# RMSNorm with GELU in float32: the stores of the output moved from ScalarE's hardware queue to GpSimd's software queue

## The chip, the cores and the metric

The kernel runs on one core of a Trainium2 chip. The metric is device time in microseconds (us); each figure is the median of several executions, with lowest and highest behind it where that matters. A single core has no second die to be compared with, so an execution is called fast or slow only by this: slow means more than 1.5% above the fastest execution of the same kernel. "The profile" is one execution recorded by the hardware profiler.

## The reference

```python
def reference(x, gamma, eps):            # x: 8 x 1024 x 2048 float32
    rms = np.sqrt(np.mean(x ** 2, axis=-1, keepdims=True) + eps)
    out = gamma * x / rms
    return 0.5 * out * (1 + np.tanh(np.sqrt(2 / np.pi) * (out + 0.044715 * out ** 3)))
```

The input has 67.11 MB and so has the output. Each row of 2048 numbers needs one sum of squares, a factor and one GELU.

## The kernel before

The 8192 rows are cut into G = 16 tiles of 128 partitions by 4 rows (4 MB each). Six buffers ("slots") hold them, and a tile is computed in place: load, squares on ScalarE, reciprocal root on GpSimd, multiplication by gamma on VectorE, GELU on ScalarE, store. A tile's row of 4 x 2048 numbers is contiguous on both sides, 32 KB.

```python
    slot = [sbuf.tile([P, R, D], FP32, name=f"slot{i}") for i in range(SLOTS)]   # SLOTS = 6
    store_pieces = {G - 1: [(0, 2), (2, 2)]}       # only the last tile is stored in two halves

    def load(g):
        nc.sync.dma_start(out=slot[g % SLOTS], in_=x3[g])                        # line 61

    def gelu_store(g):
        for r, n in store_pieces.get(g, [(0, R)]):
            for q in range(r, r + n):
                nc.scalar.activation(..., func=ACT.Gelu_apprx_tanh,              # line 101
                                     scale=rstd[:, g, q : q + 1])
            nc.scalar.dma_start(                                                 # line 105
                out=o3[g, :, r : r + n, :], in_=slot[g % SLOTS][:, r : r + n, :]
            )
    ...
        for g in range(G + 1):
            if g < G:
                squares(g); inverse_rms(g); scale(g)    # ScalarE line 65; GpSimd; VectorE line 75
            if g:
                gelu_store(g - 1)
                if g - 1 + SLOTS < G:
                    load(g - 1 + SLOTS)                 # waits until the slot has been stored
```

Of the kernel before, what the change touches and what calls it, by code (L numbers as in the profile page):

```python
# [1 line left out]

# [4 lines left out]

FP32 = mybir.dt.float32
ALU = mybir.AluOpType
ACT = mybir.ActivationFunctionType  # L10

P = 128
ROWS = 4
SLOTS = 6

GW = 128


@with_exitstack
def kernel(  # L20
    ctx: ExitStack,
    tc: tile.TileContext,
    x: bass.AP,
    gamma: bass.AP,
    eps: bass.AP,
    out: bass.AP,
):




    nc = tc.nc
    D = x.shape[-1]
    R = ROWS
    eps_f = float(eps)
    x3 = x.rearrange("b s d -> (b s) d").rearrange("(g p r) d -> g p r d", p=P, r=R)
    o3 = out.rearrange("b s d -> (b s) d").rearrange("(g p r) d -> g p r d", p=P, r=R)
    G = x3.shape[0]

    sbuf = ctx.enter_context(tc.tile_pool(name="sbuf", bufs=1))  # L40
    psum = ctx.enter_context(
        tc.tile_pool(name="psum", bufs=1, space=bass.MemoryType.PSUM)
    )
    slot = [sbuf.tile([P, R, D], FP32, name=f"slot{i}") for i in range(SLOTS)]
    gamma_row = sbuf.tile([1, D // GW, GW + 16], FP32, name="gamma_row")
    ones = sbuf.tile([1, P], FP32, name="ones")
    warm = sbuf.tile([1, 1], FP32, name="warm")
    power = sbuf.tile([P, R], FP32, name="power")
    ssq = sbuf.tile([P, G, R], FP32, name="ssq")
    rstd = sbuf.tile([P, G, R], FP32, name="rstd")  # L50
    ms = sbuf.tile([P, R], FP32, name="ms")
    y = sbuf.tile([P, R], FP32, name="y")
    z = sbuf.tile([P, R], FP32, name="z")
    gamma_ps = psum.tile([P, D], FP32, name="gamma_ps")
    junk = psum.tile([P, D], FP32, name="junk")

    store_pieces = {G - 1: [(0, 2), (2, 2)]}
    scale_pieces = {G - 1: [(0, 1), (1, 1), (2, 1), (3, 1)]}

    def load(g):  # L60
        nc.sync.dma_start(out=slot[g % SLOTS], in_=x3[g])  # L61

    def squares(g):
        for r in range(R):
            nc.scalar.activation(  # L65
                out=junk,
                in_=slot[g % SLOTS][:, r, :],
                func=ACT.Square,
                accum_out=ssq[:, g, r : r + 1],
            )  # L70

    def scale(g):
        for r, n in scale_pieces.get(g, [(0, R)]):
            rows = slot[g % SLOTS][:, r : r + n, :]
            nc.vector.tensor_tensor(  # L75
                out=rows,
                in0=rows,
                in1=gamma_ps.unsqueeze(1).to_broadcast([P, n, D]),
                op=ALU.mult,
            )  # L80

    def inverse_rms(g):

        v = nc.gpsimd
        v.tensor_scalar(  # L85
            out=ms, in0=ssq[:, g, :], scalar1=1.0 / D, scalar2=eps_f,
            op0=ALU.mult, op1=ALU.add,
        )
        v.tensor_tensor(out=y, in0=ms, in1=power, op=ALU.pow)  # L89
        v.tensor_tensor(out=z, in0=y, in1=y, op=ALU.mult)  # L90
        v.tensor_tensor(out=z, in0=z, in1=ms, op=ALU.mult)  # L91
        v.tensor_scalar(  # L92
            out=z, in0=z, scalar1=-0.5, scalar2=1.5, op0=ALU.mult, op1=ALU.add
        )
        v.tensor_tensor(out=rstd[:, g, :], in0=z, in1=y, op=ALU.mult)  # L95
# [4 lines that stand above are left out]
                row = slot[g % SLOTS][:, q, :]  # L100
                nc.scalar.activation(  # L101
                    out=row, in_=row, func=ACT.Gelu_apprx_tanh,
                    scale=rstd[:, g, q : q + 1],
                )
            nc.scalar.dma_start(  # L105
                out=o3[g, :, r : r + n, :], in_=slot[g % SLOTS][:, r : r + n, :]
            )

    with tc.manual_schedule():
        for g in range(SLOTS):  # L110
            load(g)
        nc.scalar.dma_start(
            out=gamma_row[:, :, 0:GW],
            in_=gamma.rearrange("(o a b) -> o a b", o=1, b=GW),
        )
        nc.gpsimd.memset(power, -0.5)  # L116
        nc.vector.memset(warm, 0.0)  # L117
        nc.vector.memset(ones, 1.0)  # L118
        nc.scalar.activation(out=warm, in_=warm, func=ACT.Gelu_apprx_tanh)  # L119
        for k in range(0, D, 512):  # L120
            nc.tensor.matmul(  # L121
                out=gamma_ps[:, k : k + 512],
                lhsT=ones,
                rhs=gamma_row[:, k // GW : (k + 512) // GW, 0:GW],
                start=True,
                stop=True,
            )
        for g in range(G + 1):
            if g < G:
                squares(g)  # L130
                inverse_rms(g)
                scale(g)
# [3 lines that stand above are left out]
                    load(g - 1 + SLOTS)  # L136


# [1 line left out]
_INS = ['x', 'gamma', 'eps']  # L140
_OUTS = [((8, 1024, 2048), 'float32')]

_NUMBERS = {'eps': 9.999999747378752e-06}


# [26 lines left out]
```

## Time and profile before

| what | before |
|---|---|
| time | 317.68 us (317.36 to 317.83, 3 runs) |
| span of the profiled execution | 316.9 us |
| rate of the DMA engines, 100 to 260 us | 432 GB/s |
| ScalarE (ACT) busy | 79% |
| GpSimd (POOL) busy | 10% |
| last load landed | 276.2 us |

The table is to be read from the DMA rate: all 16 DMA engines are busy from the first microseconds to 313 us, and the bytes divided by the rate give the time.

### The profile page before, as it was taken

Reading aid. Unit: us, or ns where it says so; the run is one execution under the profiler, and the core shown is the slowest. Engines: PE = TensorE matmul, PEld = TensorE weight load, DVE = VectorE, ACT = ScalarE, POOL = GpSimd, SP = SyncE. Lnnn points to the kernel's source line nnn. Section 1 sums busy time; section 2 is a strip of 40 time slices with the busy share of each in tenths; the row PEclk is TensorE's granted clock in tenths of the full one; section 3 lists DMA queues with packets and bytes.
Section 4 is the critical chain, followed back from the end, with each engine's and each line's share of the span. In section 5 each row is a group of like instructions: output and inputs, shape, how many; then the busy total and the mean of one; then the engine's idle time right before and its main releaser. Section 6 shows DMA issues by size and latency. Waiting matters only on the chain.

```text
span 316.9 us, 473 instructions
## 1 busy us (share of the span) xinstructions
PE 7.2 (2%) x8; PEld 2.5 (1%) x8; DVE 139.4 (44%) x21; ACT 251.1 (79%) x194; POOL 32.3 (10%) x101
## 2 busy tenths in 40 slices
PE   0900000000000000000000000000000000000000
PEld 0300000000000000000000000000000000000000
DVE  0038909090919191732808246091550905582000
ACT  1379999999999997959689595995959859599800
POOL 0020102020202020202002020020200102001000
DMA  8999999999999999999999999999999999999995
GB/s 328 414 451 426 434 393 459 401 459 402 459 405 455 426 434 431 430 434 426 438 426 455 410 455 418 443 426 430 434 430 435 422 459 405 459 414 447 422 420 230
DMA packets 4787, 134.25 MB, mean 424 GB/s; under 512 B 544, under 2 KB 560, under 8 KB 560
## 3 DMA queue, kind: packets, MB, share of 16 engines
q1 hardware_dynamic: 2304, 67.11, 49.5%
q10 hardware_dynamic: 2480, 67.12, 49.1%
q14 instruction: 3, 0.02, 0.0%
HBM read 67.12 MB, written 67.11 MB: 424 GB/s over the span
## 4 chain that ended last, share of the span: by engine, by line
DMA 56%; ACT 33%; issue 5%; ACTq 1%; SPq 0%
DMA slot<-in_x_dram 30%; DMA out_dram<-slot 26%; ACT slot L101 19%; ACT junk L65 14%; ACTq L105 1%; SPq L61 0%; ACTq L101 0%; ACTq L65 0%
## 5 line engine op out<-in xcount | busy, mean ns | idle before, releaser
L75 DVE TENSOR_TENSOR slot<-slot,gamma_ps 128x8192 f32<-128x8192 f32 (+1 forms) x19 | 139.2, 7340 | 147.0 <-ACT junk L65 147.0
L65 ACT ACTIVATE junk<-slot 128x2048 f32<-128x2048 f32 x64 | 120.4, 1881 | 47.3 <-DMA slot<-in_x_dram 43.7
L101 ACT ACTIVATE slot<-slot,rstd 128x2048 f32<-128x2048 f32 x64 | 122.8, 1989 | 0.9 <-ACT slot L101 0.9
L85 POOL TENSOR_SCALAR ms<-ssq 128x4 f32<-128x4 f32 x16 | 3.1, 194 | 247.5 <-ACT junk L65 247.5
L89 POOL TENSOR_TENSOR y<-ms,power 128x4 f32<-128x4 f32 x16 | 16.1, 1009 | 1.3
L65 ACT ACTIVATION_READ_ACCUMULATOR junk<-slot 128x1 f32 x64 | 12.0, 188 | 0.0
L121 PE MATMUL gamma_ps<-gamma_row,ones 1*128 1x512 f32 x8 | 7.2, 1072 | 8.4 <-DMA gamma_row<-in_gamma_dram 8.4
L95 POOL TENSOR_TENSOR rstd<-z,y 128x4 f32<-128x4 f32 x16 | 3.2, 201 | 1.3
L91 POOL TENSOR_TENSOR z<-z,ms 128x4 f32<-128x4 f32 x16 | 3.2, 201 | 1.3
L90 POOL TENSOR_TENSOR z<-y 128x4 f32<-128x4 f32 x16 | 3.2, 199 | 1.3
L92 POOL TENSOR_SCALAR z<-z 128x4 f32<-128x4 f32 x16 | 3.1, 194 | 1.4
L121 PEld LDWEIGHTS gamma_ps<-gamma_row,ones 1*128 1x128 f32 x8 | 2.5, 325 | 11.5 <-issue 11.5
L119 ACT ACT_TABLE_LOAD x1 | 1.3, 1283 | 1.3 <-PEq L153 1.3
L117 DVE MEMSET warm<- 1x1 f32 x1 | 0.1, 59 | 0.8 <-PEq L153 0.8
L119 ACT ACTIVATE warm<-warm 1x1 f32<-1x1 f32 x1 | 0.2, 202 | 0.0
L118 DVE MEMSET ones<- 1x128 f32 x1 | 0.2, 165 | 0.0
L116 POOL MEMSET power<- 128x4 f32 x1 | 0.1, 102 | 0.3 <-POOLq L153 0.3
L153 POOL MEMSET const-float32-0.0<- 128x1 f32 x1 | 0.1, 99 | 0.2 <-issue 0.2
L153 POOL MEMSET const-bfloat16-1.0<- 128x1 bf16 x1 | 0.1, 102 | 0.0
L153 POOL MEMSET const-uint8-127<- 128x1 uint8 x1 | 0.1, 102 | 0.0
L153 POOL MEMSET const-float32-1.0<- 128x1 f32 x1 | 0.1, 99 | 0.0
## 6 DMA issues: line engine op xcount, KB each, us to landing
slot<-in_x_dram SPq DMA_DIRECT2D x16, 4096.0 KB, 37.1
out_dram<-slot ACTq DMA_DIRECT2D x15, 4096.0 KB, 38.6
out_dram<-slot ACTq DMA_DIRECT2D x2, 2048.0 KB, 15.0
gamma_row<-in_gamma_dram ACTq DMA_DIRECT2D x1, 8.0 KB, 7.5
```

Source lines behind the costliest of these rows:

```text
L65: nc.scalar.activation(out=junk, in_=slot[g % SLOTS][:, r, :], func=ACT.Square, accum_out=ssq[:, g, r : r + 1],)
L75: nc.vector.tensor_tensor(out=rows, in0=rows, in1=gamma_ps.unsqueeze(1).to_broadcast([P, n, D]), op=ALU.mult,)
L85: v.tensor_scalar(out=ms, in0=ssq[:, g, :], scalar1=1.0 / D, scalar2=eps_f, op0=ALU.mult, op1=ALU.add,)
L89: v.tensor_tensor(out=y, in0=ms, in1=power, op=ALU.pow)
L90: v.tensor_tensor(out=z, in0=y, in1=y, op=ALU.mult)
L91: v.tensor_tensor(out=z, in0=z, in1=ms, op=ALU.mult)
L92: v.tensor_scalar(out=z, in0=z, scalar1=-0.5, scalar2=1.5, op0=ALU.mult, op1=ALU.add)
L95: v.tensor_tensor(out=rstd[:, g, :], in0=z, in1=y, op=ALU.mult)
L101: nc.scalar.activation(out=row, in_=row, func=ACT.Gelu_apprx_tanh, scale=rstd[:, g, q : q + 1],)
L105: nc.scalar.dma_start(out=o3[g, :, r : r + n, :], in_=slot[g % SLOTS][:, r : r + n, :])
L119: nc.scalar.activation(out=warm, in_=warm, func=ACT.Gelu_apprx_tanh)
L121: nc.tensor.matmul(out=gamma_ps[:, k : k + 512], lhsT=ones, rhs=gamma_row[:, k // GW : (k + 512) // GW, 0:GW], start=True, stop=True,)
```

## The change

The intent is to relieve ScalarE, the busiest compute engine, of issuing 17 stores (0.34 us each), and to let GpSimd, which is 10% busy, issue them by its software queue.

```diff
@@ gelu_store
-            nc.scalar.dma_start(
+            nc.gpsimd.dma_start(
                 out=o3[g, :, r : r + n, :], in_=slot[g % SLOTS][:, r : r + n, :]
             )
```

## The prediction

> **What bounds the kernel now.** I first looked at the DMA rows of the page, because the two tile streams are equal and large (67.11 MB in, 67.11 MB out).
>
> ```profile
> DMA  8999999999999999999999999999999999999995
> q1 hardware_dynamic: 2304, 67.11, 49.5%
> q10 hardware_dynamic: 2480, 67.12, 49.1%
> HBM read 67.12 MB, written 67.11 MB: 424 GB/s over the span
> DMA 56%; ACT 33%; issue 5%; ACTq 1%; SPq 0%
> ```
>
> The first row is the busy share of the 16 DMA engines in 40 slices: all are at 90% or more, but for the first and the last. q1 is the load queue (issued by SyncE), q10 the store queue (issued by ScalarE), each with half of the engines' time, together 98.6% of the span. The last row is the chain that ended last; it runs mostly through loads and stores. ScalarE is second, 79% busy, so I asked next whether the rate depends on the mixture of loads and stores, with busy time by stretches (stretch, its length, five engines, clock, DMA share, GB/s):
>
> ```profile
> 0.00:8.00 8.00, 0.00 (x0) 0.00 (x0) 0.22 (x2) 1.49 (x2) 0.29 (x5) 1.00 0.86 329
> 8.00:23.00 15.00, 7.16 (x8) 2.48 (x8) 1.73 (x1) 8.11 (x9) 1.43 (x4) 1.00 0.97 419
> 100.00:260.00 160.00, 0.00 (x0) 0.00 (x0) 73.66 (x9) 130.75 (x101) 15.97 (x48) 1.00 1.00 432
> 277.00:300.00 23.00, 0.00 (x0) 0.00 (x0) 8.88 (x4) 22.02 (x16) 2.00 (x6) 1.00 1.00 433
> 300.00:313.00 13.00, 0.00 (x0) 0.00 (x0) 0.00 (x0) 0.61 (x1) 0.00 (x0) 1.00 0.98 418
> 313.00:317.00 4.00, 0.00 (x0) 0.00 (x0) 0.00 (x0) 0.00 (x0) 0.00 (x0) 1.00 0.06 25
> ```
>
> From 100 to 260 us loads and stores share the engines, from 277 us there are only stores; the rate is 432 and 433 GB/s. The mixture does not matter. The span can be rebuilt from this: 134.25 MB at 433 GB/s is 310.0 us; the first 8 us lose 8 x 104/433 = 1.9; the next 15 lose 15 x 14/433 = 0.5; from 300 to 313 us 13 x 15/433 = 0.5; and the last 3.9 us move what takes 0.2, so 3.7 is tail. The sum is 316.6 against a measured span of 316.9 us. Nothing but bytes and the two ends is left in it.
>
> Third, who waits. These are ScalarE's and the load queue's waits (us in total, times, longest), and the time from issue to landing of stores and loads issued between 140 and 260 us:
>
> ```profile
> ACT junk L65 <- DMA slot<-in_x_dram: 43.7, 11, 10.3
> SPq L61 <- DMA out_dram<-slot: 222.0, 10, 50.7
> SPq L167 <- DMA out_dram<-slot: 39.6, 1, 39.6
> ...
> slot<-in_x_dram SPq DMA_DIRECT2D x6, 4096.0 KB, 37.0
> out_dram<-slot ACTq DMA_DIRECT2D x6, 4096.0 KB, 44.3
> ```
>
> ScalarE waits 43.7 us for loads: it is not the bound. A tile at 433 GB/s needs 4.194/433 = 9.7 us, or 19.4 beside an equal stream; 37.0 and 44.3 us to landing therefore mean that about two tiles of each kind are always queued. The end of the timeline:
>
> ```profile
> 276.24 1.88 ACT L65 ACTIVATE junk<-slot 128x2048 f32<-128x2048 f32 x1 [3.66 <-DMA slot<-in_x_dram]
> 284.26 7.67 ACT L101 ACTIVATE slot<-slot,rstd 128x2048 f32<-128x2048 f32 x4
> 284.44 0.19 POOL L85 TENSOR_SCALAR ms<-ssq 128x4 f32<-128x4 f32 x1 [16.93 <-ACT junk L65]
> 291.96 0.34 ACTq L105 DMA_DIRECT2D out_dram<-slot  x1
> 296.32 0.34 ACTq L105 DMA_DIRECT2D out_dram<-slot  x1
> 300.64 0.34 ACTq L105 DMA_DIRECT2D out_dram<-slot  x1
> ```
>
> The last load lands at 276.2, ScalarE then works for 24.4 us, and issues the last half tile at 300.64. SyncE's last wait above ends at 276.2 + 39.6 = 315.8, the landing of that store, 15.2 us after issue. A half tile alone needs 2.097/433 = 4.8 us plus about 2 us at the end: so it stood behind some 8 us of earlier stores. That 8 us is the slack in the tail.
>
> **What the Trainium skill says.** (1) The page "DMA: Bandwidth & Descriptors", section "Issuing engines are not separate DMA queues": transfers from scalar, sync and gpsimd run on the same 16 engines and interleave, and spreading them saves only issue time. The trace agrees as far as it goes: q1 and q10 each took half. (2) Same page, "Queues, rings and completion order": an engine goes round its queues packet by packet. The even split at packets of equal size (2304 and 2480 records for the same bytes) agrees. If the software queue framed its packets otherwise, the split would change; no run yet shows that. (3) Same page, "Latency and other measured facts": first byte after about 1 us by the software path against about 0.6; and engines 7 and 15 are usually slower, with the software rings in SBUF as a best guess. In the trace, which has no software queue, all engines run out of work between 313 and 314 us together (share 0.96, then 0.16), so no engine lags. (4) "SBUF — State Buffer", section "Who interferes with whom": VectorE blocks GpSimd when it uses the shared ports, in two-port modes or with two inputs in SBUF. Here the multiply has its second input in PSUM and takes 8.69 us for 8192 elements, and GpSimd's small operations run beside it without delay (194 to 201 ns, at every group). So descriptor writing should not starve.
>
> **The change part by part.** *Removed from ScalarE:* 17 issues of 0.34 us, about 0.42 with the gaps around them, 7.1 us in all. Fourteen of these lie in front of groups where ScalarE waits for a load or has tiles queued for storing; the DMA engines have work throughout, so they buy nothing. The last three bring the final issue forward by at most 2 x 0.42 = 0.8 us (the last issue itself remains, elsewhere), and that store then stands 0.8 us longer in the queue. Gain: 0.
>
> *Added on GpSimd:* 17 descriptor generations in software. The order of instructions shows each store after the reciprocal root of the next group (store of group g-1 behind the root of g), and the next root needs squares that ScalarE starts only after the GELU that the store waits for. So between a store becoming ready and the next root lie four squares, 4 x 2.04 = 8.1 us; a generation of 1 to 2 us (estimate, from the page's 1 us to the first byte) fits. The root itself takes 2.4 us (284.44 to 286.85 in the last group), and the GELU that uses it comes 7 us or more after. GpSimd goes from 32.3 us busy to some 50 to 65. On the path: 0.
>
> *Moved:* each store starts 1 us or so later, its slot comes free 1 us later, and the load into it is issued later. With about two tiles of each kind queued, no engine runs dry: 0. Each wait of a store on its semaphore goes back eight stores, long landed.
>
> *At the end:* the store is 8 us behind in the queue, so the 1 us of generation hides; completion by software may add some tenths. *At the start:* the first store comes at 38.6 us, while loads fill the engines until about 60; gamma stays where it was: 0.
>
> Sum: 0 on the middle, +0.3 us for the end and small disturbance: 317.7 + 0.3 = 318.0 us.
>
> **The rivals.** *A: the software queue is slower at moving bytes* (shorter descriptors, or rings that slow single engines). Tiles are spread evenly, so the slowest engine sets the rate. For it: the remark on engines 7 and 15. Against it: rows of 32 KB give 128 data records for 4 MB, for which fetching some bytes of descriptor each is little. If the stores ran 3% slower, half of the bytes, 310/2 x 0.03 = 4.7 us: 322 us. *B: the split tilts to the stores.* Then loads land later; total bytes stay, but the 8 us of tail slack shrink. At worst, all but the last two stores' 8.4 MB are written before the last load lands: (134.25 - 8.4)/433 + 2.4 = 293 us, then 24.4 of ScalarE and some 7 for the half tile: 324.5 us, 2% slower. *C: the split tilts to the loads.* Stores pile up, but six slots bound the pile, the engines stay full, and the time stays at 317 to 318. *D: GpSimd becomes a bound,* if one generation took over 8 us; it would then hold up roots too, and past 16 us a group everything. Nothing speaks for this. *E: ScalarE's saved 7 us count.* Only if DMA were not full; at most 1 us, 316.7.
>
> **Range and chances.** The bytes set a floor near 316, as no part of the change moves fewer or faster: over 2% faster would be below 311.3, under the 310.0 of pure transfer plus any tail; chance 0.01. A and B reach past 324.0 only in their strong forms, together 0.09. The rest, 0.90, is within 2%. The range is lopsided: 315.9 to 322.0.
>
> **What would show it right or wrong.** Right: q10 all but empty, a software queue with 67.11 MB near 49%, 432 GB/s in the middle, a DMA row full to the end, ScalarE's waits for loads grown by about the 6 to 7 us it saved, span within 1.5 us. Step by step: the duration of the new GpSimd work (1 to 2 us), the root still done well before its GELU, and the last load landing near 276. Wrong by A: a middle rate below 425, or a tail in which few engines still work. Wrong by B: time to landing of stores near 10 to 20 us, last load after 284, engines idle behind it. Wrong by D: GpSimd above 100 us busy and ScalarE waiting for it.

## The result, and the profile after

The changed kernel took 336.56 us (331.91 to 342.68, 4 runs: 333.73 and 331.91 fast, 339.39 and 342.68 slow), the kernel before 317.52 us in the same rounds. The ratio is 1.0481, with a 95% interval of 1.0429 to 1.0532: slower. A ratio here is the mean time of one kernel's fast runs over that of the other's of the same rounds, so it is not quite the ratio of the medians quoted. The profiled execution is a fast one (333.73 us).

The page of the kernel after (span; busy tenths of the DMA engines in 40 slices; queues with packets, MB and share of the engines' time; rate; chain that ended last; the new work on GpSimd with total, mean ns and wait; issues with the median time to landing):

```profile
span 332.0 us, 498 instructions
...
DMA  8999999999999999999999999999999999792996
...
q1 hardware_dynamic: 2304, 67.11, 48.1%
q0 software_dynamic: 2448, 67.11, 47.9%
...
HBM read 67.12 MB, written 67.11 MB: 404 GB/s over the span
...
DMA 59%; ACT 26%; issue 8%; POOL 1%; POOLq 0%; SPq 0%; ACTq 0%
...
L105 POOL DMA_DIRECT2D out_dram<-slot x17 | 10.7, 628 | 86.7 <-ACT slot L101 86.7
...
slot<-in_x_dram SPq DMA_DIRECT2D x16, 4096.0 KB, 41.4
out_dram<-slot POOLq DMA_DIRECT2D x15, 4096.0 KB, 45.3
```

The bytes are the same, the two streams still share the engines evenly, and the new work on GpSimd is cheap: 628 ns for a store, and it is GpSimd that waits for ScalarE. Loads and stores both take longer to land (37.1 and 38.6 us before). And the DMA row has a hole near its end, a slice at 7 and one at 2, where the kernel before was full.

Busy time by stretches of the kernel after (stretch, length, five engines, clock, DMA share, GB/s):

```profile
60.00:280.00 220.00, 0.00 (x0) 0.00 (x0) 95.56 (x11) 172.86 (x133) 29.05 (x77) 1.00 1.00 423
100.00:260.00 160.00, 0.00 (x0) 0.00 (x0) 63.46 (x9) 118.58 (x94) 19.79 (x52) 1.00 1.00 421
280.00:290.00 10.00, 0.00 (x0) 0.00 (x0) 8.69 (x1) 7.83 (x6) 2.64 (x7) 1.00 0.85 360
290.00:298.00 8.00, 0.00 (x0) 0.00 (x0) 4.19 (x2) 6.13 (x7) 0.00 (x0) 1.00 1.01 434
298.00:310.00 12.00, 0.00 (x0) 0.00 (x0) 4.69 (x3) 12.00 (x8) 2.64 (x7) 1.00 0.31 134
310.00:328.00 18.00, 0.00 (x0) 0.00 (x0) 0.00 (x0) 5.01 (x3) 1.06 (x2) 1.00 0.99 422
328.00:332.00 4.00, 0.00 (x0) 0.00 (x0) 0.00 (x0) 0.00 (x0) 0.00 (x0) 1.00 0.18 74
```

The same stretch of the kernel before, for comparison:

```profile
60.00:280.00 220.00, 0.00 (x0) 0.00 (x0) 105.98 (x13) 185.95 (x143) 23.97 (x72) 1.00 1.00 433
```

These lines hold the whole 15.1 us. Against the 433 GB/s of before, the stretch from 60 to 280 us loses 220 x 10/433 = 5.1 us, with the engines *busy* all the time (share 1.00): packets take longer. From 280 to 290 us the loss is 10 x 73/433 = 1.7 us, and from 298 to 310 us it is 12 x 299/433 = 8.3 us, with the engines *idle* (share 0.31). The sum is 15.1 us, the difference of the two spans.

Waits of ScalarE, GpSimd and the load queue after (us in total, times, longest):

```profile
POOL out_dram L105 <- ACT slot L101: 86.7, 17, 5.4
ACT junk L65 <- DMA slot<-in_x_dram: 61.9, 12, 10.1
...
SPq L61 <- DMA out_dram<-slot: 243.4, 10, 59.6
SPq L167 <- DMA out_dram<-slot: 78.5, 2, 74.0
```

ScalarE's waits for loads grew from 43.7 to 61.9 us. The load queue's waits for stores grew too, 222.0 to 243.4 us: slots come free late.

The end of the timeline after (start, duration, engine, line, operation, [idle time before, and what ended it]):

```profile
291.78 1.88 ACT L65 ACTIVATE junk<-slot 128x2048 f32<-128x2048 f32 x1 [3.95 <-DMA slot<-in_x_dram]
...
299.79 15.23 ACT L101 ACTIVATE slot<-slot,rstd 128x2048 f32<-128x2048 f32 x8
299.98 0.19 POOL L85 TENSOR_SCALAR ms<-ssq 128x4 f32<-128x4 f32 x1 [11.22 <-ACT junk L65]
...
307.74 0.63 POOL L105 DMA_DIRECT2D out_dram<-slot  x1 [5.35 <-ACT slot L101]
311.53 0.53 POOL L105 DMA_DIRECT2D out_dram<-slot  x1 [3.15 <-ACT slot L101]
315.31 0.53 POOL L105 DMA_DIRECT2D out_dram<-slot  x1 [3.25 <-ACT slot L101]
```

The last load lands at 291.7 us, 15.5 us later than before. From there everything is a fixed sequence: 8.0 us of squares and 7.9 us of GELU until the store of tile 14 is issued at 307.74, then that tile and the two halves of the last, 8.39 MB, onto engines that have little else: 8.39/433 = 19.4 us. Together with the ends it is 332.0 - 291.8 = 40.2 us from the last load to the end. Before it was 316.9 - 276.2 = 40.7 us. So the late load explains all of the difference, and the question is why the load is late.

**The packets one by one.** The trace also has a record for each packet of the DMA engines: start, duration, size and queue, but not the engine. I rebuilt the 16 engines as chains, since the next packet of an engine starts 3 to 4 ns before the end of the last one's record (where packets of two engines end together, two chains may be swapped). An undisturbed packet of 32 KB takes exactly 1213 ns, one of 16 KB 611 ns and one of 8 KB 309 ns. What a packet takes above that I call its stretch. In the kernel before, 19 packets that start between 60 and 280 us are stretched by more than 4%; all stretch together, smaller ones included, is 4.0 us. In the kernel after it is 390 packets (half of them by more than 0.17 us) and 89.7 us (loads 42.6, stores 47.1). The window leaves out a stretch that both kernels have: from 40 to 45 us, as the first store comes in, one or two load packets of each engine stretch (10.1 us in all before, 13.1 after). Spread over 16 engines that is 5.6 us, which answers to the 5.1 us lost in the rate above. The stretch is not spread evenly, though. The 16 chains of the kernel after:

```
first software   stretch of stores, us      stretch of      last load
store packet     60-280 us  (60-120 us)     loads, us       ends at, us
43.18             5.5       (3.9)           3.2             278.4
43.18            15.3       (4.0)           1.0             291.4
43.20            15.0       (3.8)           0.1             290.1
44.43             0.6       (0.3)           1.3             275.0
44.44             8.3       (0.2)           1.3             289.0
the other 11:     0 to 0.6  (0 to 0.2)      1.2 to 5.3      275.0 to 279.7
```

Three engines lose some 14 to 15 us each (the first and the fifth chain are most likely one engine's, swapped halfway). A load is spread over all 16 engines and has landed only when the slowest of them is through. So three late engines out of 16 delay every tile, though the mean rate falls by only 2%. The records say so without any rebuilding too: each engine ends its share of a load with a packet of 4 bytes, and for the last load thirteen of these end at 275.0 to 279.7 us and three at 289.0, 290.1 and 291.4 (all sixteen at 274.1 to 275.8 in the kernel before). The table shows one more thing: the engines that lose are those that began their first software store one packet earlier than the rest (43.2 against 44.4 to 44.8 us), which puts them out of step with the others. Out of step can also be seen without chains, in the number of engines that load at a moment: 0 or 16 when all are in step. In the kernel after, from 62 to 100 us, it was 3 or 13 for 29% of the time, and 0 or 16 for 6%.

### The profile page after: what moved, and what is told of

Its sections match the earlier page's. It is cut to its first block, busy times and chain, and to the rows that moved or that the text cites. A ratio compares the mean times of both kernels' runs of the same rounds, so it can differ in the third digit from the quotient of the medians.

```text
span 332.0 us, 498 instructions
## 1 busy us (share of the span) xinstructions
PE 7.2 (2%) x8; PEld 2.5 (1%) x8; DVE 139.4 (42%) x21; ACT 250.3 (75%) x194; POOL 43.1 (13%) x118
## 3 DMA queue, kind: packets, MB, share of 16 engines
q1 hardware_dynamic: 2304, 67.11, 48.1%
q0 software_dynamic: 2448, 67.11, 47.9%
## 4 chain that ended last, share of the span: by engine, by line
DMA 59%; ACT 26%; issue 8%; POOL 1%; POOLq 0%; SPq 0%; ACTq 0%
DMA slot<-in_x_dram 31%; DMA out_dram<-slot 28%; ACT junk L65 13%; ACT slot L101 13%; POOL out_dram L105 0%; POOL y L89 0%; POOLq L167 0%; SPq L61 0%; POOL z L91 0%; POOL z L90 0%; POOL rstd L95 0%; POOL ms L85 0%; POOL z L92 0%; POOLq L105 0%; ACTq L65 0%
## 5 line engine op out<-in xcount | busy, mean ns | idle before, releaser
L65 ACT ACTIVATE junk<-slot 128x2048 f32<-128x2048 f32 x64 | 120.3, 1880 | 63.4 <-DMA slot<-in_x_dram 61.9
L105 POOL DMA_DIRECT2D out_dram<-slot x17 | 10.7, 628 | 86.7 <-ACT slot L101 86.7
L89 POOL TENSOR_TENSOR y<-ms,power 128x4 f32<-128x4 f32 x16 | 16.5, 1032 | 1.3
## 6 DMA issues: line engine op xcount, KB each, us to landing
out_dram<-slot POOLq DMA_DIRECT2D x15, 4096.0 KB, 45.3
```

Of the source, the lines that this page charges most:

```text
L65: nc.scalar.activation(out=junk, in_=slot[g % SLOTS][:, r, :], func=ACT.Square, accum_out=ssq[:, g, r : r + 1],)
L89: v.tensor_tensor(out=y, in0=ms, in1=power, op=ALU.pow)
L105: nc.gpsimd.dma_start(out=o3[g, :, r : r + n, :], in_=slot[g % SLOTS][:, r : r + n, :])
```

## The experiments

Theory at the start (*ring*): something of the software path, such as fetching its descriptors, slows a few engines. Rival (*step*): the software queue only puts some engines out of step with the others, and out-of-step engines stretch each other's packets, whichever queue issues. Further rivals came from the results: *fixed engines*, *packet length*, *alignment of the rows*. "Stretch" below is always the sum for packets starting between 60 and 280 us, loads plus stores. The times of the kernel before in the same rounds were 317.57, 317.99, 317.41, 317.43, 317.58 and 317.47 us (medians), in the order of the groups 1 to 6 of runs.

### Group 1: is it the software queue, and which engines?

**tags_sw** is the kernel after with 14 tiny transfers over 2 to 15 partitions near the end, meant to mark which chain is which engine.

```diff
+            if g == G - 1 and r == 0:
+                tags([8, 7, 15, 14, 13, 12, 11, 10, 9, 6, 5, 4, 3, 2])   # n rows of 64 bytes, nc.scalar
```

> The changed kernel plus 14 tiny hardware transfers near its end, of 2 to 15 partitions[...], so that the packet records tell which chain of packets is which engine. In the changed kernel three chains of 16 lost 14 to 17 us, on stores alone (packets of 1213 ns stretched by 100 to 600 ns), and 13 chains some 3 to 6 us. Theory 'fixed engines': the slow ones are always the same engines, and by the Trainium skill's remark 7 and 15 should be among them; the last load lands at 288 to 296 us as before the tags. Theory 'drift' (engines that happen to fall out of step collide): any engines, in another number than three. Time near 332 to 345 us in either case.

It took 333.61 us (one look). Three chains were slow again, with 87.4 us of stretch, and the early ones were three too. The marks ran from 303 to 325 us, when many engines were idle, so they could not be tied to a chain: inconclusive on which engines.

**hw_tiny_sw** is the kernel before with a tiny software transfer beside each store.

```diff
+            nc.gpsimd.dma_start(out=tiny_b, in_=tiny_a)     # 128 rows of 512 bytes
             nc.scalar.dma_start(
```

> The kernel before (stores on ScalarE's hardware queue) with one small software transfer from GpSimd beside each store: 128 rows of 512 bytes inside SBUF, as many descriptors as a store has, 1 MB more in all. Theory 'descriptors in SBUF': writing and fetching the software descriptors is what slows some engines, so this costs much of the 15 us: 327 us or more. Rival 'the store's own data must come through the software queue': 317 to 320 us (1 MB more, about 2.5 us at 433 GB/s), and no engine's stores are stretched.

321.17 us (321.06 to 321.34), ratio 1.0101 (1.0074 to 1.0128), with 11.5 us of stretch. Of the extra 3.6 us the added 1.1 MB need 2.6 by the rate. Software descriptors in as many numbers as the stores of the kernel after have do not bring the slowness.

**hw_offset3** is the kernel before with one tiny hardware transfer over 3 partitions, to set three engines out of step.

```diff
+            if g == 6:
+                tags([3])
```

> The kernel before with a single tiny hardware transfer on 3 partitions at about 103 us on the store queue: it takes one turn of the store queue on three engines, so that their stores stand one packet apart from the other thirteen's, as in the changed kernel, with no software queue at all. Theory 'drift': the three (or the thirteen) engines' packets now stretch, and the time rises to 325 us or more. Theory 'software queue': nothing happens, 317 to 319 us.

318.76 us (317.48 to 319.55), ratio 1.002 (0.9977 to 1.0064), stretch 4.3 us: nothing. But the packet records show that the edit did not do what it was meant to. The mark ran at 140 us, not at 103, and afterwards (142 to 160 us) 0 or 16 engines loaded for 31% of the time, about as before it (34%), and 3 or 13 for 11%: no three engines were set a packet apart. So this run does not test the rival, which was tried harder in group 3.

**sw_first8** issues the first eight stores by software and the others by hardware.

```diff
-            nc.gpsimd.dma_start(
+            (nc.gpsimd if g < 8 else nc.scalar).dma_start(
```

> Software stores for groups 0 to 7 only, hardware stores from ScalarE for groups 8 to 15. Theory 'software queue': stretched packets only until the last software store has landed, at about 205 us, then 1213 ns again; about half of the cost, 322 to 327 us. Theory 'drift': the engines stay out of step, the stretching goes on to the last load and the cost is nearly whole, 330 us or more.

344.69 us (338.80 to 351.13; one fast, three slow runs): slower than the kernel after, which neither theory expected. The profiled (slow) run has 122.4 us of stretch, the most of all; four engines ended their last load at 301.4 to 304.6 us, the others at 285.3 or before. Its queues from 182 to 200 us:

```profile
q0 software_dynamic: 91, 2.82, 40.9%
q1 hardware_dynamic: 81, 2.52, 33.4%
q10 hardware_dynamic: 59, 1.93, 25.5%
```

For a while the old software stores and the new hardware stores are queued together, and three queues share the engines, so the loads get a third in place of a half. That may be a cost of its own, so the time says nothing clean about half the number of software stores. What the run does show: from 225 to 255 us, after the last software packet had ended (225.4 us), packets still stretched (9.1 us of loads and 4.4 us of hardware stores), and it died away after that. So the stretch can outlast the software packets for a time.

### Group 2: fixed engines, packets, the end

**tags_early** is the kernel after with four marks, at a time when the engines are full.

```diff
+            if g == 2:
+                tags([7, 8, 15, 4])
```

> The changed kernel plus four tiny hardware transfers of 7, 8, 15 and 4 partitions at about 31 to 39 us, while only loads run: in the chain of packets of one engine, engines 0 to 3 carry four of them, 4 to 6 three, 7 two, 8 to 14 one, 15 none. (In the run with tags at the end the tags ran while most engines were idle, and could not be put to chains.) Theory 'fixed engines' with the Trainium skill's guess: of the two or three chains whose stores stretch from 80 us on, one carries two tags (engine 7) and one carries none (engine 15). If the ring's place in SBUF were not the cause, the slow chains carry other numbers. Time 332 to 345 us.

329.83 us (one look), with 95.7 us of stretch: more than the kernel after, in less time, but spread over five engines and not three. Five engines were early and five stretched; they carried 3, 4, 4, 1 and 0 of the four marks. If a transfer over n partitions goes to the engines 0 to n-1, these were engines out of 4 to 6, 0 to 3 twice, 8 to 14, and 15. Engine 7 would carry two marks, and no slow chain had two. So the slow engines are no fixed pair: *fixed engines* falls.

**sw_pad** pads each row of 2048 numbers in the slot by 64 bytes. A tile then moves in packets of 8 KB, four times as many descriptors, in both directions. **hw_pad** is the same with hardware stores, as a control.

```diff
-    slot = [sbuf.tile([P, R, D], FP32, name=f"slot{i}") for i in range(SLOTS)]
+    slot = [sbuf.tile([P, R, D + 16], FP32, name=f"slot{i}") for i in range(SLOTS)]
```

> The changed kernel with the rows of a slot padded by 64 bytes in SBUF, so that every descriptor, of loads and of stores, moves 8 KB and not 32 KB: four times the descriptors, the same bytes, the same transfers. If a slow engine's stretch is a cost of fetching each software descriptor, some 170 ns on each store packet of the slow engines, it grows up to fourfold, by 45 us: 360 us or more. If it goes with bytes or with the software queue as such, the time stays at 332 to 345 us.

> The control of the run before: the kernel before with the same padding, stores on ScalarE's hardware queue. Shorter descriptors alone should cost little here: 317 to 322 us on every theory. If it is slower than that, the difference to it, not to the kernel before, is what the software queue costs at 8 KB.

sw_pad took 321.45 us (321.18 to 321.77), ratio 1.0102 (1.0074 to 1.0131); hw_pad 320.89 us (320.77 to 320.92), ratio 1.0083 (1.005 to 1.0116). The stretches of 220 to 260 us, sw_pad first and then hw_pad:

```profile
220.00:260.00 40.00, 0.00 (x0) 0.00 (x0) 17.38 (x2) 31.95 (x27) 5.52 (x14) 1.00 1.01 428
```

```profile
220.00:260.00 40.00, 0.00 (x0) 0.00 (x0) 17.38 (x2) 31.34 (x25) 3.98 (x12) 1.00 1.01 427
```

Both move 427 to 428 GB/s, and the stretch is 0.5 and 0.7 us. With four times the descriptors *ring* expected a much slower kernel, and it expected wrongly: the slowness is gone. Between the software and the hardware version remain 321.45/320.89, 0.2%. What has changed is either the packet length or the alignment.

**sw_last3** issues only the stores of the last three tiles by software.

```diff
-            nc.gpsimd.dma_start(
+            (nc.gpsimd if g >= 13 else nc.scalar).dma_start(
```

> Software stores for the last three groups only (13, 14 and 15); all others by hardware. In the changed kernel's records the slow engines' stores are stretched only while loads run too, and are 1213 ns again once the loads are over, at about 280 us. If the stretch needs loads beside it, these software stores, nearly all issued when the last load has landed or is about to, cost nothing: 316.5 to 319 us. If software stores are slow by themselves, 3/16 of the cost or more shows: 320.5 us or more.

317.49 us (317.45 to 317.97), ratio 0.9981 (0.9953 to 1.0009), stretch 1.7 us. The software path costs nothing measurable at the end of the kernel: not its generation, not its completion.

### Group 3: the rival, pushed harder

**hw_shift** is the kernel before with three larger hardware copies at g == 1 which give 4, 8 and 12 engines extra packets, before the first stores.

```diff
+            if g == 1:
+                for i, n in enumerate((4, 8, 12)):
+                    nc.scalar.dma_start(out=o3[G - 1 - i, 0:n, 0:1, :], in_=x3[0, 0:n, 0:1, :])
```

> The kernel before, all stores on ScalarE's hardware queue, with three small hardware copies of 4, 8 and 12 rows of 8 KB at about 15 to 20 us (into output rows that the last groups overwrite): [...]engines stand 0, 0.3, 0.6 or 0.9 us apart, a part of a 1.213 us packet. In the kernel before nearly all engines load at once and then store at once; in the changed kernel they don't. Theory 'loss of step': out of step, 32 KB packets of loads and stores collide and stretch, whatever queue issued them: stretched packets from 60 us on, and 323 us or more. Theory 'software queue': stretching needs packets from the software queue: none here, 317 to 320 us.

318.38 us (318.22 to 318.56), ratio 1.0024 (1.0006 to 1.0043), stretch 4.5 us, and 433 GB/s from 100 to 260 us. The packet records show that the engines were out of step: from 60 to 260 us the number of engines that load at a moment varied about as little (standard deviation 3.5) as in the kernel after (3.4), against 5.6 in the kernel before, where nearly all load together and then store together. Out of step by hardware alone brings no stretch in this profiled execution: *step*, in its plain form, falls.

**sw_first1** issues only the very first store by software.

```diff
-            nc.gpsimd.dma_start(
+            (nc.gpsimd if g < 1 else nc.scalar).dma_start(
```

> Only the store of group 0 is issued by software, all others by hardware. Theory 'loss of step': one software store at 38.7 us can put the engines out of step, and nothing brings them back, so the stretching goes on with hardware stores alone: 323 us or more. In the run with eight software stores the packets went on stretching for 30 us after the last software packet. Theory 'software queue': no stretched packet after the only software store has landed at about 63 us, 316.5 to 319 us.

318.46 us (318.07 to 319.50), ratio 1.0037 (1.0007 to 1.0067), stretch 3.1 us. Again three engines began the first store early, yet nothing stretched afterwards. But the engines were soon back in step: 0 or 16 of them loaded for 50% of the time from 62 to 100 us. So one early store leaves no stretch behind; what hardware stores would do on engines that stay one packet ahead, this run does not show.

### Group 4: packet length, one queue at a time

**sw_16k_two** pads between the halves of a slot row and stores each tile in two transfers, so that loads and stores both go in 16 KB packets. **hw_16k_one** is the padded layout with one hardware store, as a control, also at 16 KB.

```diff
-    slot = [sbuf.tile([P, R, D], FP32, name=f"slot{i}") for i in range(SLOTS)]
+    slot = [sbuf.tile([P, 2, 2 * D + 16], FP32, name=f"slot{i}") for i in range(SLOTS)]
...
+            for a in range(r, r + n, 2):
+                nc.gpsimd.dma_start(
+                    out=o3[g, :, a : a + 2, :].rearrange("p r d -> p (r d)"), in_=view(g, a, 2))
```

> Software stores in two transfers a group, each of plain shape (128 x 4096), and slots padded by 64 bytes between their halves, so that loads and stores both move 16 KB packets. Theory 'length': half the packet, half or less of the stretch: between the 321.5 of the 8 KB run and the 332 to 342 of the changed kernel, say 321 to 328 us. Theory 'shape' (the padded run was healed because the store's access pattern was folded to 512 rows): the stretch stays whole, 330 us or more.

> The control for the 16 KB runs: hardware stores from ScalarE, slots padded between halves, so that loads and stores both move 16 KB packets. 317 to 321 us on every theory, no stretched packet.

sw_16k_two took 320.21 us (320.20 to 320.24), ratio 1.0082 (1.006 to 1.0104), stretch 1.1 us; hw_16k_one 318.84 us (318.77 to 319.26), ratio 1.0041 (1.0022 to 1.0061), stretch 1.6 us. The rate and the last load of sw_16k_two:

```profile
220.00:260.00 40.00, 0.00 (x0) 0.00 (x0) 18.29 (x5) 32.78 (x27) 6.38 (x16) 1.00 1.01 432
```

```profile
273.99 1.88 ACT L71 ACTIVATE junk<-slot 128x2048 f32<-128x2048 f32 x1 [3.17 <-DMA slot<-in_x_dram]
```

The software queue moves 432 GB/s here, and the last load lands at 274.0 us, even earlier than in the kernel before.

**sw_store2** is the kernel after with every store in two transfers (16 KB packets) and whole loads (32 KB), **sw_load2** the reverse. Neither has padding.

```diff
 sw_store2
-        for r, n in store_pieces.get(g, [(0, R)]):
+        for r, n in store_pieces.get(g, [(0, 2), (2, 2)]):
 sw_load2
-        nc.sync.dma_start(out=slot[g % SLOTS], in_=x3[g])
+        for r in (0, 2):
+            nc.sync.dma_start(out=slot[g % SLOTS][:, r : r + 2, :], in_=x3[g, :, r : r + 2, :])
```

> The changed kernel with each store as two software transfers of half a row group, so that store packets are 16 KB and load packets stay 32 KB; an engine that goes round its queues packet by packet then gives loads two thirds of the time while both wait. If the length of the store's packets is what stretches, 318 to 326 us; if only loads' packets matter, 330 us or more. The uneven split alone should cost nothing (rival C of the prediction: loads come early, stores pile up behind them).

> The changed kernel with each load as two hardware transfers, so that load packets are 16 KB and store packets stay 32 KB; stores then get two thirds of the time while both wait. If the load's packets being long is what stretches the stores, 318 to 326 us; if it is the store's length, 330 us or more. The split alone may cost up to 324.5 us by rival B of the prediction, so the packet records decide, not the time.

sw_store2 took 327.18 us (325.62 to 328.65), ratio 1.0301 (1.0251 to 1.035); sw_load2 331.63 us (327.16 to 333.00), ratio 1.0378 (1.0284 to 1.0472). Stretch: 51.8 us in the first (37.5 of it on the 32 KB loads), 30.5 us in the second (24.5 of it on the 16 KB loads). Shorter packets on one queue alone leave a good part of the stretch. The times from issue to landing show another effect, sw_store2 first and then sw_load2:

```profile
slot<-in_x_dram SPq DMA_DIRECT2D x16, 4096.0 KB, 20.4
out_dram<-slot POOLq DMA_DIRECT2D x32, 2048.0 KB, 40.9
```

```profile
slot<-in_x_dram SPq DMA_DIRECT2D x32, 2048.0 KB, 58.6
out_dram<-slot POOLq DMA_DIRECT2D x15, 4096.0 KB, 19.3
```

The queue with the longer packets gets more of the engines: its transfers land in about 20 us, the other queue's pile up. So these two runs carry a tilted split as well as the stretch, and their times cannot be read as the stretch alone: in sw_store2 the last load lands early, at 273.9 us, and the loss sits in the stores that pile up behind it.

### Group 5: length or alignment

**sw_both2** joins the two edits of sw_store2 and sw_load2: 16 KB packets both ways, without padding. **sw_slotpad** is the other way round: 32 KB packets, but a 64-byte spacer after each slot.

```diff
 sw_slotpad
+        slot.append(sbuf.tile([P, R, D], FP32, name=f"slot{i}"))
+        sbuf.tile([P, 16], FP32, name=f"spacer{i}")
```

> Software stores and hardware loads both in two plain transfers a group, no padding: 16 KB packets on both queues. Theory 'length': as good as the padded 16 KB run, 318 to 322 us, no stretched packet. Theory 'padding': stretched packets and 326 us or more.

> The changed kernel with an unused tile of 64 bytes after every slot, so that the slots no longer start at multiples of 32 KB in a partition; packets stay 32 KB on both queues. Theory 'length': 330 to 343 us and stretched packets as in the changed kernel. Theory 'padding': 317 to 321 us, no stretched packet.

sw_both2 took 320.70 us (320.14 to 320.98), ratio 1.0095 (1.0072 to 1.0118), stretch 1.2 us. sw_slotpad took 332.80 us (338.66, 335.57 and 330.03 slow, 321.02 fast), and its profiled execution, a slow one, has 59.5 us of stretch. So packets of 32 KB can stretch without the alignment, and packets of 16 KB do not stretch with it: the packet length is what matters. But the 321.02 us belong to the range expected for *padding*, and no execution of the kernel after was that fast (330.62 at the least, of nine). Alignment may change how often the stretch comes; this stays open. sw_slotpad's profile is instructive: one engine alone was early, lost 20.3 us on its stores, and had its last load at 296.3 us. From 60 to 280 us the mean rate was 427 GB/s:

```profile
60.00:280.00 220.00, 0.00 (x0) 0.00 (x0) 95.56 (x11) 168.00 (x131) 29.17 (x77) 1.00 1.01 427
```

By that rate the kernel should lose 3 us; one late engine of 16 made it 20.

**after_again** runs the kernel after again, later (on chip 5; the chip of the first result is not on record).

> The changed kernel again, beside the two runs above: 330 to 343 us as before, some 200 stretched load packets and some 200 stretched store packets between 60 and 280 us.

332.59 us (330.62 to 341.13), ratio 1.0493 (1.0443 to 1.0543): the result repeats. The profiled execution was the slow one of 341.13 us, with 96.5 us of stretch. It had two early engines, with 23 us each and their last loads at 298.7 and 298.1 us. The timeline of its end:

```profile
299.17 1.88 ACT L65 ACTIVATE junk<-slot 128x2048 f32<-128x2048 f32 x1 [3.69 <-DMA slot<-in_x_dram]
```

Its span is 339.4 us: again 40.2 us after the last load, as in sw_slotpad and tags_early. In the profiled runs with software stores throughout and whole 32 KB packets, few early engines went with large losses (1 or 2: 338.66 and 341.13 us), more with smaller ones (3: 333.73 and 333.61; 5: 329.83). In each of these five as many engines ended their last load late (by the packets of 4 bytes) as had begun the first software store early. Only five executions were profiled, so this fits the spread between executions but is not shown to be its cause.

### Group 6: an open end

**hw_offset13** is hw_offset3 with 13 partitions, the mirror image of three early engines.

```diff
-                tags([3])
+                tags([13])
```

> The kernel before with a single tiny hardware transfer on 13 partitions at about 103 us on the store queue: it takes one turn of the store queue on thirteen engines, so that three engines' stores run one turn ahead of the others', as in the changed kernel's profiled run, without any software queue. Theory 'order is enough': the three engines' stores stretch from then on, 322 us or more. Theory 'order and software queue': nothing stretches, 317 to 319.5 us.

321.46 us, ratio 1.0156 (1.0096 to 1.0215), verdict unclear: 317.47 and 320.23 fast, 324.37 and 322.68 slow. The profiled execution was that of 317.47 us, which has only 3.4 us of stretch; there, too, the mark (at 140 us) set no engines apart, as 0 or 16 engines loaded for 40% of the time before it and 36% after. The other three were not profiled. So it may be that engines out of step can stretch packets on hardware queues too, in some executions. hw_shift, whose engines were well out of step, did not show it. This stays open.

## Why the prediction was wrong, and what was right in it

The prediction said 318.0 us, 315.9 to 322.0; the result is 336.56. The class "within 2%" with chance 0.90 was wrong, "slower" had 0.09.

**Right.** The generation of descriptors is off the path. It took 628 ns, less than the "1 to 2 us" estimated, GpSimd went from 32.3 to 43.1 us busy (predicted 50 to 65), and GpSimd waits for ScalarE. The step that takes the power still takes 1032 ns (1009 before), and in the last group the root is done at 302.4 us, before the GELU that uses it. sw_last3 shows the end's share directly: 0.9981. The 7 us saved on ScalarE bought nothing, as argued, and the split stayed even (48.1 and 47.9%).

**The step that failed first** is the "0 on the middle" of the sum. Its ground, under *Moved*, was "With about two tiles of each kind queued, no engine runs dry: 0": it asked only whether the engines have work, and took the 432 GB/s in the middle as a property of the DMA engines which the issuing queue cannot touch. The engines did have work (share 1.00 from 60 to 280 us). In place of the 0 the runs showed packets of 32 KB that stretch, most of all on one to five engines, a middle at 421 GB/s and a last load 15.5 us later. Rival A had the right outline ("rings that slow single engines", "the slowest engine sets the rate", and as a sign "a middle rate below 425, or a tail in which few engines still work"). But it was sized by "3% slower" on the mean and given little weight since "rows of 32 KB give 128 data records", few and large. The reverse held: with 8 KB packets, four times as many descriptors, the stretch is gone (sw_pad), and with 16 KB too (sw_both2). And the size of a slow engine's effect comes from its own delay (15 us), not from the mean (5 us).

**The second step that failed** is "That 8 us is the slack in the tail". It looked at the last half tile alone, which stood behind 8 us of earlier stores. But these earlier stores, tile 14 and the first half of tile 15, are themselves issued only after the last load has landed, since the squares of tile 15 precede the GELU of tile 14 on ScalarE. So 16 us of ScalarE and 8.39 MB hang behind the last load: 16.0 + 19.4 us and the ends, measured as 40.2 us in the kernel after, when nothing else was left. Before it was 40.7, and the shortest distance that a hardware version showed is 37.7 us (sw_first1: last load at 278.7, span 316.4). The true slack was therefore about 3 us or less, and the 15.5 us of a late load passed into the time as 15.1. The same term is wrong in rival B: "24.4 of ScalarE and some 7 for the half tile" is 31 us where the runs show 40, so its worst case of 324.5 should have read 293 + 40 = 333 us, which is where the kernel ended. Had this been worked out, the range would have reached further, whatever made the load late.

**The signs.** Wrong: "a DMA row full to the end", "432 GB/s in the middle", the last load "near 276" (291.7), waits for loads up by 6 to 7 us (up by 18.2). Of the sign for B, "last load after 284, engines idle behind it" came true, but not its cause: stores took 45.3 us to landing (38.6 before), not 10 to 20, so no tilt to the stores made the load late.

**What is shown and what is not.** Shown: the late load makes the loss; the load is late since a few engines' packets stretch; in the profiled runs this came only with software-issued stores over much of the kernel (in sw_first8 it outlasted them by 30 us) together with packets of 32 KB on at least one queue, and it goes when both queues use 16 or 8 KB packets (ratio 1.0095 and 1.0102, of which the smaller packets alone cost 0.4% and 0.8%, by the padded controls with hardware stores). Excluded as the cause by runs: the number of software descriptors, fixed engines, generation and completion at the end; alignment is not needed for it. Not shown: *why* a long packet stretches on an engine that began early. Being out of step alone did not do it in hw_shift, but in no profiled run did a few engines stay one whole packet ahead of the others with hardware queues alone, and the slow executions of hw_offset13 leave a doubt. No version beat the kernel before; sw_last3 equals it (0.9981, 0.9953 to 1.0009), as the bytes set the time.

## What to carry to other kernels

When the DMA engines are the bound, do not read only the mean rate: a transfer lands with its slowest engine, so look at packet durations, and at the distance from the last load to the end, which is the sum of everything that can only begin then. If stores must be issued from GpSimd beside a full stream of loads, use packets of 16 KB or less on both queues (such versions cost 0.8 to 1.0% here, against 4.8%), or leave the large stores on a hardware queue. And keep the packets of two queues equal in length, as the longer ones take the larger share.

## What the Trainium skill lacked or had wrong

- "DMA: Bandwidth & Descriptors", section "Issuing engines are not separate DMA queues": it says that transfers run on the same engines and interleave whichever engine started them, and that using several issuers saves only sequencer time. The section knows no cost of the choice of issuer. Here it cost 4.8% (ratio 1.0481, and 1.0493 again in a later round), with the bytes and the packet sizes unchanged.
- Same page, section "Latency and other measured facts": engines 7 and 15 as the slow ones, with the descriptor rings as a best guess. By the marks of tags_early, if they are numbered as assumed there, the slow engines were others as well as 15 (five of them, none with engine 7's marks). Their number varied from 1 to 5 between profiled executions, and with four times the descriptors the stretch was gone (0.5 us, and 321.45 against 336.56 us), so as a cost of each descriptor the guess does not explain this.
- Same page, section "Queues, rings and completion order": the round agrees, but the page has a turn of some 9 to 17 descriptors, while here a turn was one record of the trace, one row of 32 KB (1039 of the 1047 turns in the rebuilt chains of the kernel before, 100 to 180 us). What follows is not in that section: halving the packets of one queue only cuts that queue's share of the engines. Transfers with 32 and 16 KB packets landed in 20.4 and 40.9 us (sw_store2).
- No page has it that 32 KB packets can stretch, stores and loads alike, when a software queue stores beside a stream of loads: 1213 ns undisturbed, a median of 175 ns more on 390 packets, 89.7 us in all from 60 to 280 us, against 4.0 us with hardware stores.
